# Both parts of a unit of weights in one tile, the parts at byte offsets chosen by kind of unit

## The chip, the core and the metric

The kernel runs on one core of a Trainium2 chip. The metric is the device time of one execution in microseconds (us); before the change the median of three runs is 968.93 us (968.75 to 969.19).

## What is computed

One layer of a bidirectional encoder on 256 tokens of width 2048, in float32. Cut to what matters here:

```python
h = _rmsnorm(x, norm1_g)
proj = h @ w_in                                  # 2048 x 3072: q (12 heads), k, v (4 heads), u (512)
a = _rmsnorm(_window_attention(q, k, v, sink), attn_out_g)
f = _rmsnorm(_fourier_mix(u, w_fourier), fourier_out_g)
x = x + jnp.concatenate([a, f], axis=-1) @ w_out           # 2048 x 2048
up = _rmsnorm(x, norm2_g) @ w_up                           # 2048 x 11008
act = gelu(conv3(gate) + dw_b) * val                       # width 5504
x = x + act @ w_down                                       # 5504 x 2048
return _rmsnorm(x, normf_g)
```

Nearly all the arithmetic is in the products with `w_in`, `w_out`, `w_up` and `w_down`.

## The kernel before

**Units of weights.** All weights are read once, in units of 128 partitions x 2048 float32 (1 MB): 24 of `w_in` (4 for u, 4 for v, 16 for the heads of q and k), 16 of `w_out`, 86 of `w_up` (gate and value of 43 tiles of 128 features), and the units of `w_down`. A unit is loaded by SyncE's queue into one of three `raw` buffers (`load`, L134), and `split_parts` (L149) makes two tiles of it in the type that TensorE reads in one pass: `hi`, the rounded value, written by ScalarE (L163), and `lo`, the rest `raw - hi`, written by VectorE (L164). Each has three buffers. Activations are held in the same way as two parts. A product then takes three matmuls (hi by hi, hi by the activations' rest, lo by hi), accumulated in one PSUM bank.

**Three forms of product.** A matmul holds one operand of 128 x 128 in the array (loaded by a separate instruction, PEld in the profile, while the matmul before it still runs) and streams the other through it.

- *Weights that stay* (`still_weights`, L308; heads of q and k, and all of `w_up`; 102 units). For each of 16 blocks of 128 rows, the hi part of the weights stays and 512 columns stream by (both parts of the activations side by side, L313), then the lo part stays and 256 columns stream by (L314). What streams is `hT` (`hU` after the second norm).
- *Weights that stream* (`moving_weights`, L296, lines L302 to L304): u and v, with `hT` staying; `w_out`, with the `cat` tiles staying; the units of `w_down` behind the last groups (`ps_l`), with `act` tiles staying.
- *Products* (`by_parts`, L1005, lines L1009 to L1011): the first 32 tiles of `w_down` in four groups of features, by a scheme with seven products of sums of blocks for each half of the columns, 56 in all. Here too the weights stream and an operand `op_*` stays. `split_product` (L897) makes hi and lo of them (L905, L906) in the same two rings of tiles as the units.

The last four units (`split_last`, L1131) have their own tiles.

**Order.** It is written out by hand. `unit(i, work)` (L345) issues the matmuls of unit i, then the small work that was put `beside` it, then the split of unit i + 2, which also issues the load of a unit three further on (L166); from the second norm on, `ff_step` (L936) does the same along `items`, in which products stand alternately with units of `w_up`. So when unit i is in TensorE, unit i + 1 is split, and i + 2 is being split into the buffer that unit i - 1 has left.

**Where the tiles lie.** Pools and tiles are laid out in each partition in the order in which they are opened: the pool `base` (with `hT`), then `wp` (`raw`, `hi`, `lo`, a scratch tile), then the pools of the stages. In the built program every tile of `raw`, `hi` and `lo`, the `cat`, `act` and `op_*` tiles start 32 bytes behind a multiple of 128 bytes, and the four `hT` tiles 96 bytes behind one. All slices that a matmul reads are whole multiples of 512 bytes further on, so an operand keeps its tile's distance. In this text a matmul's *offset* is the distance between the starts of the operand that streams and of the operand that is loaded under it, modulo 128 bytes: 0 for `w_out`, the late units of `w_down` and the products, 64 for u and v and for all weights that stay.

Of the kernel before, what the change touches and what calls it, by code (L numbers as in the profile page):

```python
# [9 lines left out]
F32R = mybir.dt.float32r  # L10
# [3 lines left out]
P = 128  # L14
# [33 lines left out]
N_U, N_V, N_QK = 0, 4, 8  # L48
# [7 lines left out]
LAST = list(range(40, NF))  # L56
# [27 lines left out]
def block_kernel(  # L84
# [22 lines left out]
    wp = ctx.enter_context(tc.tile_pool(name="wp", bufs=1))  # L107
# [3 lines left out]
    def f32(ap):  # L111
        return ap.bitcast(F32)
# [2 lines left out]
        return pool.tile([P, 512], F32, tag=pool.name, name=name)  # L115


    units = [(w_in[i], 2048) for i in range(24)] + [(w_out[i], 2048) for i in range(16)]
    n_front = len(units)
    items, up_index = ff_items(), {}  # L120
    for n, it in enumerate(items):
        if it[0] == "product":
            continue
        up_index[n] = len(units)
        if it[0] in ("gate", "val"):
            units.append((w_up[2 * it[1] + (it[0] == "val")], 2048))
        elif it[0] == "down":
            units.append((w_down_late[4 * it[1] + it[2]], 2048))
        else:
            units.append((w_down_last[it[1]], 512 * len(LAST)))  # L130
    RAW = 3
    raws, halves = {}, {}

    def load(i, pieces=1):  # L134
        if i < len(units) and i not in raws:
            src, n = units[i]
            raws[i] = wp.tile([P, 2048], F32, tag="raw", name=f"raw{i}", bufs=RAW)
            m = n // pieces
            for p in range(pieces):
                s = slice(p * m, (p + 1) * m)  # L140
                nc.sync.dma_start(raws[i][:, s], src[:, s])
                yield

    def split(i, pieces=1):

        for _ in split_parts(i, pieces):
            pass

    def split_parts(i, pieces):  # L149
        if i >= len(units):  # L150
            return
        n = units[i][1]
        raw = raws[i]
        hi = wp.tile([P, 2048], F32R, tag="hi", name=f"hi{i}", bufs=3)
        lo = wp.tile([P, 2048], F32R, tag="lo", name=f"lo{i}", bufs=3)
        halves[i] = (hi, lo)
        m = n // pieces
        for p in range(pieces):
            s = slice(p * m, (p + 1) * m)
            if i == 0 and p == 0:  # L160
                nc.vector.tensor_copy(hi[:, s], raw[:, s])
            else:
                nc.scalar.activation(hi[:, s], raw[:, s], AF.Copy)  # L163
            nc.vector.tensor_tensor(lo[:, s], raw[:, s], f32(hi[:, s]), ALU.subtract)  # L164
            yield
        for _ in load(i + RAW):  # L166
            pass
        load_more(i + RAW)
# [24 lines left out]
    nc.scalar.activation(warm[:, 0:1], warm[:, 1:2], AF.Copy)  # L193

    first = load(0, 4)
    nc.scalar.dma_start(vec[:, 0:NK], vecs[:, 0:NK])
    load_x(0, 0, S)
# [5 lines left out]
    next(first)  # L203
    load_x(2)
    second = load(1, 4)
    next(second)
    next(second)
# [15 lines left out]
    def load_more(i):  # L223

        if i == 4:
            for c in range(2):
                nc.sync.dma_start(xs[c], x[:, :, c * 512 : (c + 1) * 512])
        if i == 5:
            for c in range(2, 4):
                nc.sync.dma_start(xs[c], x[:, :, c * 512 : (c + 1) * 512])  # L230
        if i == 6:
            nc.sync.dma_start(chan, c_chan)
            nc.sync.dma_start(wfs, wf)
            nc.sync.dma_start(pos, c_pos)
        if i == 7:
            nc.sync.dma_start(vec[:, NK:V_N], vecs[:, NK:V_N])
            nc.sync.dma_start(rel, c_rel)
# [115 lines left out]
    for c in range(4):  # L353
        t = base.tile([P, 4, 512], F32R, tag=f"hT{c}", name=f"hT{c}")
        hT.append(t)
    ps_u = [bank(mm, f"ps_u{b}") for b in range(2)]
    for k in range(NK):
        c, q = k // 4, k % 4
        if q == 0:
            parts = split_parts(c, 4 if c < 2 else 2)  # L360
        split_scaled(hk(k), xTc[k // 2][:, (k % 2) * S : (k % 2 + 1) * S], vcol(V_G1 + k))
        next(parts, None)
        hi, lo = halves[c]
        for b in range(2):
            moving_weights(
                hi, lo, 512, [k], hk, b, ps_u[b], k == 0, k == NK - 1, q0=q
            )
        if q == 3:
            for _ in parts:
                pass  # L370
            del halves[c]
# [384 lines left out]
    for n, (c, kq) in enumerate(OUT_ORDER):  # L756
        i = N_OUT + n
# [35 lines left out]
    parts = {}  # L793
# [91 lines left out]
    def weights_of(g, c, w):  # L885
        return w_down[(g * 2 + c) * 4 + "abcd".index(w)]

    def ring_load():
        if ring_next[0] < len(ring):
            key = ring[ring_next[0]]  # L890
            ring_next[0] += 1
            ring_tiles[key] = fp.tile([P, 2048], F32, tag="rawd", name="rawd%d%d%s" % key)
            nc.sync.dma_start(ring_tiles[key], weights_of(*key))
# [3 lines left out]
    def split_product(g, c, p):  # L897

        raw = {w: ring_tiles.get((g, c, w)) for w in "abcd"}
        x = ring_tiles["x"]  # L900
        src = {"P1": raw["a"], "N3": raw["d"], "P7": raw["b"], "P2": raw["c"]}.get(p, x)
        hi = wp.tile([P, 2048], F32R, tag="hi", name=f"hi_{p}_{g}{c}", bufs=3)
        lo = wp.tile([P, 2048], F32R, tag="lo", name=f"lo_{p}_{g}{c}", bufs=3)
        halves["product", g, c, p] = (hi, lo)
        nc.scalar.activation(hi, src, AF.Copy)  # L905
        nc.vector.tensor_tensor(lo, src, f32(hi), ALU.subtract)  # L906
        if p in ("P1", "P7", "N3", "P2"):
            ring_load()
        elif p == "N5":
            nc.gpsimd.dma_start(x, weights_of(g, c, "d"), accum_op=ALU.add)  # L910
        elif p == "P6":
            nc.gpsimd.dma_start(x, weights_of(g, c, "c"), accum_op=ALU.add)
        elif p == "N4" and (g, c) != (N_GROUPS - 1, 1):
            pending.append(lambda: first_sums(g + c, 1 - c))

    def first_sums(g, c):

        a, b = ring_tiles[g, c, "a"], ring_tiles[g, c, "b"]
        x = ring_tiles["x"] = fp.tile([P, 2048], F32, tag="sumw", name=f"sumw{g}{c}", bufs=1)
        nc.vector.tensor_tensor(x, a, b, ALU.add)  # L920
        nc.gpsimd.dma_start(b, weights_of(g, c, "d"), accum_op=ALU.add)

    def split_item(n):
        if n >= len(items):
            return
        it = items[n]
        if n in up_index:
            split(up_index[n])
            if pending:
                pending.pop(0)()  # L930
        else:
            while pending:
                pending.pop(0)()
            split_product(*it[1:])
# [153 lines left out]
    for n, it in enumerate(items):  # L1088
# [15 lines left out]
        if it[0] == "product":  # L1104
            kind, g, c, p = it
# [9 lines left out]
        else:  # L1115
            kind, g, c = it
            hi, lo = halves.pop(up_index[n])
# [11 lines left out]
    i = up_index[n]  # L1129
# [145 lines left out]
```

## Time and profile before

| what | value |
|---|---|
| median of three runs | 968.93 us |
| span of the profiled execution (first to last instruction) | 967.9 us, so about 1.0 us lies around it |
| granted TensorE clock, mean | 0.997 of full |
| 60 to 206 us: q, k and the attention | 861 matmuls, TensorE busy all the time |
| 206 to 270 us: output projection | 308 matmuls, TensorE busy all the time |
| 270 to 860 us: `w_up` and the products | 3171 matmuls, TensorE busy all the time |
| read from memory | 208.65 MB, 218 GB/s over the span |

Times in the profile's views are microseconds unless they are marked ns. In a view that groups instructions a row has line, engine, operation, the tile written and the tiles read, shapes and count, then the group's busy time in us and the mean of one in ns, then idle time in front of it and what ended it. In a view in order of time a row begins with its start and its length. Matmuls overlap in the records: one that streams 512 columns is listed with some 390 ns although the next starts some 230 ns later. The spacing of their starts is what the time is made of, and the two differ by the same 162 ns in all the groups that are used below.

### The profile page before, as it was taken

To read this page: it belongs to the slowest core of one execution; us is meant where nothing else is said; L and a number is where in the kernel's file an instruction comes from. 1 tells how busy PE (TensorE), PEld (TensorE's weight loads), DVE (VectorE), ACT (ScalarE), POOL (GpSimd) and SP (SyncE) were. 2 spreads that over 40 slices of the span, in tenths; PEclk is the share of its full clock that TensorE was granted. 3 is DMA by queue.
4 is the path that set the end of the run, shared out by engine and by line. 5 is a ranking of instruction groups with operands and counts; after the bars stand their busy time and mean duration, and the time that the engine had idled before them with its cause. 6 is when DMAs were issued, how large, how long until landed. Compare 5 with 4: busy or idle time off the path is not lost.

```text
span 967.9 us, 12808 instructions
## 1 busy us (share of the span) xinstructions
PE 958.3 (99%) x5089; PEld 821.8 (85%) x5089; DVE 745.5 (77%) x924; ACT 537.5 (56%) x654; POOL 44.5 (5%) x59
## 2 busy tenths in 40 slices
PE   9999999999999999999999999999999999999996
PEld 7788988888888888888888888888888888888885
DVE  5668877666666679886898877988878989888674
ACT  6746666545554456655555555565555755553534
POOL 0000000000000000000000000000000000000003
PEclk9999999999999999999999999999999999999998
DMA  9844434445545675978687797776977696766532
GB/s 318 338 175 168 166 139 152 153 174 198 194 174 210 234 243 182 263 254 265 217 261 226 235 285 256 237 241 218 282 249 244 208 283 212 230 234 212 196 131 87
DMA packets 33548, 211.59 MB, mean 219 GB/s; under 512 B 3792, under 2 KB 4304, under 8 KB 9424
## 3 DMA queue, kind: packets, MB, share of 16 engines
q1 hardware_dynamic: 29744, 184.54, 51.3%
q0 software_dynamic: 3600, 26.22, 14.4%
q8 instruction: 40, 0.66, 0.3%
q14 instruction: 20, 0.16, 0.0%
q10 hardware_dynamic: 144, 0.01, 0.0%
HBM read 208.65 MB, written 2.10 MB: 218 GB/s over the span
## 4 chain that ended last, share of the span: by engine, by line
PE 95%; DMA 2%; DVE 1%; ACT 1%; issue 0%; POOL 0%; ACTq 0%; POOLq 0%; SPq 0%
PE ps_gate L313 17%; PE ps_val L313 17%; PE ps_gate L314 8%; PE ps_val L314 8%; PE ps_q L313 5%; PE ps_P L1009 3%; PE ps_P L1011 3%; PE ps_P L1010 3%; PE ps_q L314 2%; PE ps_a L304 2%; PE ps_a L303 2%; PE ps_a L302 2%; PE ps_N L1009 2%; PE ps_N L1011 2%; PE ps_N L1010 2%; DMA raw<-in_w_in 2%
## 5 line engine op out<-in xcount | busy, mean ns | idle before, releaser
L164 DVE TENSOR_TENSOR lo<-raw,hi 128x2048 fp32r<-128x2048 f32 (+3 forms) x145 | 313.0, 2158 | 59.3 <-ACT hi L163 59.3
L163 ACT ACTIVATE hi<-raw 128x2048 fp32r<-128x2048 f32 (+3 forms) x144 | 261.7, 1817 | 64.5 <-PE ps_l L303 25.4
L313 PE MATMUL ps_gate<-hU,hi 128*128 128x512 f32 x688 | 242.9, 394 | 0.0
L313 PE MATMUL ps_val<-hU,hi 128*128 128x512 f32 x688 | 242.8, 394 | 0.0
L314 PE MATMUL ps_gate<-hU,lo 128*128 128x256 f32 x688 | 193.1, 281 | 0.0
L314 PE MATMUL ps_val<-hU,lo 128*128 128x256 f32 x688 | 193.1, 281 | 0.0
L313 PEld LDWEIGHTS ps_val<-hU,hi 128*128 128x128 f32 x688 | 129.4, 188 | 29.9
L313 PEld LDWEIGHTS ps_gate<-hU,hi 128*128 128x128 f32 x688 | 129.4, 188 | 29.9
L314 PEld LDWEIGHTS ps_gate<-hU,lo 128*128 128x128 f32 x688 | 129.0, 187 | 1.1
L314 PEld LDWEIGHTS ps_val<-hU,lo 128*128 128x128 f32 x688 | 128.9, 187 | 1.1
L798 ACT ACTIVATE ft_g<-ps_gate 128x256 f32<-128x256 f32 x43 | 16.5, 383 | 127.5 <-PE ps_gate L314 127.5
L798 ACT ACTIVATE ft_v<-ps_val 128x256 f32<-128x256 f32 x43 | 16.5, 383 | 96.8 <-PE ps_val L314 96.7
L313 PE MATMUL ps_q<-hT,hi 128*128 128x512 f32 x192 | 68.5, 397 | 0.0
L314 PE MATMUL ps_q<-hT,lo 128*128 128x256 f32 x192 | 54.0, 281 | 0.0
L1009 PE MATMUL ps_P<-hi_P,op_P 128*128 128x512 f32 x128 | 50.2, 392 | 0.0
L1011 PE MATMUL ps_P<-lo_P,op_P 128*128 128x512 f32 x128 | 50.1, 391 | 0.0
L1010 PE MATMUL ps_P<-hi_P,op_P 128*128 128x512 f32 x128 | 49.8, 389 | 0.0
L906 DVE TENSOR_TENSOR lo_N<-sumw,hi_N 128x2048 fp32r<-128x2048 f32 x16 | 36.6, 2289 | 10.2 <-ACT hi_N L905 10.2
L313 PEld LDWEIGHTS ps_q<-hT,hi 128*128 128x128 f32 x192 | 36.1, 188 | 8.0
L800 DVE TENSOR_TENSOR fa_g<-ps_gate,ft_g 128x256 f32<-128x256 f32 x43 | 18.1, 421 | 29.4 <-ACT ft_g L798 29.4
L302 PE MATMUL ps_a<-hi,cat 128*128 128x512 f32 x96 | 37.8, 394 | 0.0
L1009 PE MATMUL ps_N<-hi_N,op_N 128*128 128x512 f32 x96 | 37.7, 393 | 0.0
(317 smaller groups left out, 1594.3 us busy)
## 6 DMA issues: line engine op xcount, KB each, us to landing
raw<-in_w_up SPq DMA_DIRECT2D x86, 1024.0 KB, 5.0
raw<-in_w_in SPq DMA_DIRECT2D x21, 1024.0 KB, 4.9
raw<-in_w_out SPq DMA_DIRECT2D x16, 1024.0 KB, 4.7
sumw<-in_w_down POOLq DMA_DIRECT2D x16, 1024.0 KB, 8.7
raw<-in_w_down_late SPq DMA_DIRECT2D x8, 1024.0 KB, 4.9
raw<-in_w_down_last SPq DMA_DIRECT2D x4, 768.0 KB, 4.2
raw<-in_w_in SPq DMA_DIRECT2D x8, 256.0 KB, 6.7
xs<-in_x SPq DMA_DIRECT2D x4, 512.0 KB, 10.2
```

Source lines behind the costliest of these rows:

```text
L163: nc.scalar.activation(hi[:, s], raw[:, s], AF.Copy)
L164: nc.vector.tensor_tensor(lo[:, s], raw[:, s], f32(hi[:, s]), ALU.subtract)
L302: nc.tensor.matmul(ps, ah, wh, start=first and q == q0, stop=False)
L303: nc.tensor.matmul(ps, al, wh, start=False, stop=False)
L304: nc.tensor.matmul(ps, ah, wl, start=False, stop=last and q == q0 + len(kk) - 1)
L313: nc.tensor.matmul(ps, hi[:, s], h, start=k == 0, stop=False)
L314: nc.tensor.matmul(ps[:, 0:S], lo[:, s], h[:, 0:S], start=False, stop=k == NK - 1)
L798: nc.scalar.activation(tmp, ps[:, S : 2 * S], AF.Copy)
L906: nc.vector.tensor_tensor(lo, src, f32(hi), ALU.subtract)
L1009: nc.tensor.matmul(ps, o[:, 0, p, :], hi[:, s], start=first and p == 0, stop=False)
L1010: nc.tensor.matmul(ps, o[:, 1, p, :], hi[:, s], start=False, stop=False)
L1011: nc.tensor.matmul(ps, o[:, 0, p, :], lo[:, s], start=False, stop=last and p == 3)
```

## The change

Both parts of a unit now lie in one tile of 4096 + 128 float32 (16,896 bytes) of one ring `parts` with three buffers. The hi part starts `oh` floats behind the tile's start and the lo part 2048 + `ol` floats behind it, and a table gives the two by the kind of unit. The loads and their queue, the order of the instructions on each engine, and what TensorE waits for stay the same.

```diff
-    units = [(w_in[i], 2048) for i in range(24)] + [(w_out[i], 2048) for i in range(16)]
+    units = [(w_in[i], 2048, "first" if i < N_QK else "still") for i in range(24)]
+    units += [(w_out[i], 2048, "moving") for i in range(16)]
...
-            units.append((w_up[2 * it[1] + (it[0] == "val")], 2048))
+            units.append((w_up[2 * it[1] + (it[0] == "val")], 2048, "still"))
         elif it[0] == "down":
-            units.append((w_down_late[4 * it[1] + it[2]], 2048))
+            units.append((w_down_late[4 * it[1] + it[2]], 2048, "moving"))
         else:
-            units.append((w_down_last[it[1]], 512 * len(LAST)))
+            units.append((w_down_last[it[1]], 512 * len(LAST), "moving"))
...
+    PLACES = {"still": (0, 16), "first": (16, 16), "moving": (0, 0), "product": (28, 28)}
+
+    def parts_tile(name, place):
+        t = wp.tile([P, 2 * 2048 + 128], F32R, tag="parts", name=name, bufs=3)
+        oh, ol = PLACES[place]
+        return t[:, oh : oh + 2048], t[:, 2048 + ol : 4096 + ol]
...
-        hi = wp.tile([P, 2048], F32R, tag="hi", name=f"hi{i}", bufs=3)
-        lo = wp.tile([P, 2048], F32R, tag="lo", name=f"lo{i}", bufs=3)
-        halves[i] = (hi, lo)
+        hi, lo = halves[i] = parts_tile(f"parts{i}", place)
...
-        hi = wp.tile([P, 2048], F32R, tag="hi", name=f"hi_{p}_{g}{c}", bufs=3)
-        lo = wp.tile([P, 2048], F32R, tag="lo", name=f"lo_{p}_{g}{c}", bufs=3)
-        halves["product", g, c, p] = (hi, lo)
+        hi, lo = halves["product", g, c, p] = parts_tile(f"parts_{p}_{g}{c}", "product")
```

In the built program the three tiles of the ring start 32 bytes behind a multiple of 128, as `hi` and `lo` did; `hT` stays where it was; the tiles behind the ring move by 1536 bytes, which is a multiple of 512. With the offset as defined above (stream against what is loaded under it):

| kind | where hi and lo start, modulo 128 bytes | offset before | offset after |
|---|---|---|---|
| u, v ("first") | 96, 96 (the stream) | 64 | 0 |
| weights that stay | 32, 96 (loaded under `hT` at 96) | 64, 64 | 0 where lo is loaded (under the 512 columns of L313), 64 where hi is loaded (under the 256 columns of L314) |
| `w_out`, late `w_down` ("moving") | 32, 32 (the stream) | 0 | 0 |
| products | 16, 16 (the stream) | 0 | 112 |

A buffer of hi could be written again as soon as the last matmul on hi had ended, and one of lo after the last matmul on lo. Now ScalarE waits for the last matmul on either part before it writes the tile's hi part (L163, L905); VectorE's own wait there is gone, since it waits for ScalarE anyway. 75 of TensorE's 389 semaphore signals fall away.

More of the change, by code (lines that the diff above doesn't have):

```diff
@@ L125, in block_kernel @@
         if it[0] in ("gate", "val"):
-            units.append((w_up[2 * it[1] + (it[0] == "val")], 2048))
+            units.append((w_up[2 * it[1] + (it[0] == "val")], 2048, "still"))
         elif it[0] == "down":
-            units.append((w_down_late[4 * it[1] + it[2]], 2048))
+            units.append((w_down_late[4 * it[1] + it[2]], 2048, "moving"))
         else:
-            units.append((w_down_last[it[1]], 512 * len(LAST)))
+            units.append((w_down_last[it[1]], 512 * len(LAST), "moving"))
     RAW = 3
     raws, halves = {}, {}
+    PLACES = {"still": (0, 16), "first": (16, 16), "moving": (0, 0), "product": (28, 28)}
[3 more added lines that the diff above has]
+        return t[:, oh : oh + 2048], t[:, 2048 + ol : 4096 + ol]
     def load(i, pieces=1):
         if i < len(units) and i not in raws:
-            src, n = units[i]
+            src, n, _ = units[i]
             raws[i] = wp.tile([P, 2048], F32, tag="raw", name=f"raw{i}", bufs=RAW)
@@ L151, in split_parts @@
             return
-        n = units[i][1]
+        _, n, place = units[i]
         raw = raws[i]
-        hi = wp.tile([P, 2048], F32R, tag="hi", name=f"hi{i}", bufs=3)
-        lo = wp.tile([P, 2048], F32R, tag="lo", name=f"lo{i}", bufs=3)
-        halves[i] = (hi, lo)
+        hi, lo = halves[i] = parts_tile(f"parts{i}", place)
         m = n // pieces
```

## Prediction

> **What bounds the kernel now.** First the page: busy times, TensorE's slices with its clock, and the chain of work that ended last.
>
> ```profile
> PE 958.3 (99%) x5089; PEld 821.8 (85%) x5089; DVE 745.5 (77%) x924; ACT 537.5 (56%) x654; POOL 44.5 (5%) x59
> PEclk9999999999999999999999999999999999999998
> PE 95%; DMA 2%; DVE 1%; ACT 1%; issue 0%; POOL 0%; ACTq 0%; POOLq 0%; SPq 0%
> ```
>
> TensorE is busy in 958.3 of 967.9 us at full clock, and 95% of the chain is its own work. So the time is the number of matmuls times the spacing of their starts. No matmul is added or removed; what the change can move is that spacing. The second view is therefore the list of groups by form.
>
> ```profile
> L313 PE MATMUL ps_gate<-hU,hi 128*128 128x512 f32 x688 | 242.9, 394 | 0.0
> L313 PE MATMUL ps_val<-hU,hi 128*128 128x512 f32 x688 | 242.8, 394 | 0.0
> L314 PE MATMUL ps_gate<-hU,lo 128*128 128x256 f32 x688 | 193.1, 281 | 0.0
> L313 PE MATMUL ps_q<-hT,hi 128*128 128x512 f32 x192 | 68.5, 397 | 0.0
> L313 PE MATMUL ps_k<-hT,hi 128*128 128x512 f32 x64 | 22.8, 396 | 0.0
> L303 PE MATMUL ps_v<-hi,hT 128*128 128x512 f32 x32 | 12.6, 395 | 0.0
> L304 PE MATMUL ps_v<-lo,hT 128*128 128x512 f32 x32 | 12.6, 395 | 0.0
> L303 PE MATMUL ps_l<-hi,act 128*128 128x512 f32 x64 | 24.9, 389 | 0.0
> L304 PE MATMUL ps_l<-lo,act 128*128 128x512 f32 x64 | 24.9, 389 | 0.0
> L1146 PE MATMUL ps_e<-hi,act 128*128 128x512 f32 x21 | 8.2, 389 | 0.0
> L1147 PE MATMUL ps_e<-hi,act 128*128 128x256 f32 x6 | 1.7, 283 | 0.0
> ```
>
> All rows of 512 columns do the same work, and yet ps_v takes 395 ns and ps_l 389. Lines 303 and 304 are the same code for both; what differs is where the operands lie: offset 64 for v, 0 for the late units. The weights that stay, offset 64 too, show 394 to 397. The timeline turns this into spacings.
>
> ```profile
> 33.84 0.40 PE L302 MATMUL ps_v<-hi,hT 128*128 128x512 f32 x1
> 35.94 0.39 PE L302 MATMUL ps_v<-hi,hT 128*128 128x512 f32 x1
> ...
> 866.01 0.39 PE L302 MATMUL ps_l<-hi,act 128*128 128x512 f32 x1
> 871.45 0.39 PE L302 MATMUL ps_l<-hi,act 128*128 128x512 f32 x1
> ...
> 320.98 0.39 PE L313 MATMUL ps_gate<-hU,hi 128*128 128x512 f32 x1
> 325.93 0.40 PE L313 MATMUL ps_gate<-hU,hi 128*128 128x512 f32 x1
> ...
> 374.59 0.39 PE L313 MATMUL ps_val<-hU,hi 128*128 128x512 f32 x1
> 379.48 0.40 PE L313 MATMUL ps_val<-hU,hi 128*128 128x512 f32 x1
> ```
>
> Nine matmuls of v lie between the first two rows: 2.10 / 9 = 233.3 ns each. Between the next two lie 24 of ps_l: 5.44 / 24 = 226.7 ns. The 6.7 ns between them is the 6 ns between 395 and 389, so the listed duration less 162 ns is the spacing. The last four rows bound 14 pairs (L313 and L314) each, in one code at the same places: 4.95 / 14 = 353.6 ns in a unit at 320 us and 4.89 / 14 = 349.3 ns in one at 374 us. So the pairs keep one of two spacings, and neither is the best one that the other rows allow: 226.7 ns as in ps_l, and for 256 columns 281 to 283 less 162, so 120 ns: 346.7 together.
>
> I read this as a collision in the memory of TensorE's two reads, the stream and the weight load under it, that depends on their places: offset 0 is the good case and 64 costs up to 6.7 ns for 512 columns. The other reading, that hT's tile rather than its offset is slow, would give the same rows; I hold it less likely, since hT is slow in both roles, staying (v) and streaming (L313).
>
> **The change part by part.** *Weights that stay, 1632 pairs.* While the 512 columns of L313 stream from hT (96), the lo part is loaded; it moves to 96, offset 0. While the 256 columns of L314 stream, the next hi part is loaded, still at 32: offset 64 as now. For gate and value the first goes from 394 to 389, -5 ns. L314 shows 281 at offset 64 and its like 282 to 283 at offset 0, so nothing is to be gained there; I take +1 ns, because a tighter pair keeps to 120. That is 1376 x -4 = -5.5 us. The 256 matmuls of q and k show 396 to 397, -7.5 + 1 = -6.5 ns, -1.7 us. Of this some 0.9 us isn't the placement's: the first matmul of most of these units takes longer behind the attention's transposes.
>
> ```profile
> 153.56 0.48 PE L313 MATMUL ps_q<-hT,hi 128*128 128x512 f32 x1
> 153.87 0.28 PE L314 MATMUL ps_q<-hT,lo 128*128 128x256 f32 x1
> ```
>
> This one has 310 ns to the next instead of 231, some 80 ns that stay; in all 16 units it would be 1.3 us, and I take two thirds. So q and k give -0.8 us, and this part -6.3 us. Bounds: from the spacing that each pair has to 346.7 it cannot exceed -1632 x 5 = -8.2 us by these rows; on the other side all pairs could fall to 353.6 ns, which costs those that stand at 349.3 now 4.3 ns each. If that is all units of `w_up` behind the 19 that have run by 374 us, 67 x 16 = 1072 pairs, it is +4.6 us.
>
> *u and v, 192 matmuls.* Offset 64 becomes 0: 395 to 389. For v 96 x -6 = -0.6 us. For u as much, but the beginning waits on loads (the chain's DMA 2%), which gives part back: -0.2 us. Sum -0.8 us; bounds 0 and -1.2.
>
> *w_out and the late units, 576 matmuls.* Offset 0 before and after: nothing.
>
> *Products, 672 matmuls.* The stream moves to 16, offset 112, which no matmul of 512 columns here has.
>
> ```profile
> L1009 PE MATMUL ps_P<-hi_P,op_P 128*128 128x512 f32 x128 | 50.2, 392 | 0.0
> L1010 PE MATMUL ps_P<-hi_P,op_P 128*128 128x512 f32 x128 | 49.8, 389 | 0.0
> L1011 PE MATMUL ps_P<-lo_P,op_P 128*128 128x512 f32 x128 | 50.1, 391 | 0.0
> L1009 PE MATMUL ps_N<-hi_N,op_N 128*128 128x512 f32 x96 | 37.7, 393 | 0.0
> L1010 PE MATMUL ps_N<-hi_N,op_N 128*128 128x512 f32 x96 | 37.3, 389 | 0.0
> L1011 PE MATMUL ps_N<-lo_N,op_N 128*128 128x512 f32 x96 | 37.6, 392 | 0.0
> ```
>
> The first matmuls of each product run unevenly until they settle. Against 389 that is (3 + 0 + 2) x 128 + (4 + 0 + 3) x 96 = 1.3 us in all. Offset 112 is 16 bytes from 0 and 48 from 64, so the nearest row is 389, and a quarter of the way to 395 gives 390.5, about today's mean. I take 0; bounds -1.3 us (all at 389) and 4.0 - 1.3 = +2.7 us (all at 395).
>
> *The shared tile.* ScalarE's write of the hi part now waits for the last matmul on lo, one matmul or 0.23 us later at most.
>
> ```profile
> ACT hi L163 <- PE ps_l L303: 25.4, 8, 4.0
> 865.98 1.92 ACT L163 ACTIVATE hi<-raw 128x2048 fp32r<-128x2048 f32 x1 [0.33 <-PE ps_N L1010]
> 868.83 2.28 DVE L164 TENSOR_TENSOR lo<-raw,hi 128x2048 fp32r<-128x2048 f32 x1
> ```
>
> Behind it on ScalarE stand the next unit's small works, and for it waits VectorE's lo part. In the tight place shown, hi would end at 865.98 + 0.23 + 1.92 = 868.13, and the lo part starts only at 868.83, behind VectorE's earlier work: 0.7 us are left. Elsewhere the split of unit i + 2 starts while unit i runs, and has the whole of unit i + 1 (16 pairs, 5.6 us) behind it before TensorE needs it. So nothing; without that cover it would be 0.23 us a unit. The writes at shifted places could take ScalarE and VectorE longer, and no row shows such a shift; even 5% of VectorE's 745.5 us would stay under TensorE's 958.3.
>
> Sum: -6.3 - 0.8 = -7.1 us. The profiled span of 967.9 becomes 960.8; the median lies 1.0 us above its span, so 961.8 us.
>
> The Trainium skill speaks against any effect: "TensorE: Matmul & The Clock Gate", in Part 2 on issuing a matmul, gives TensorE two independent read ports and says that loading the next weights takes no bandwidth from the running matmul. By it the sum would be 0. The two spacings of ps_v and ps_l, 233.3 and 226.7 ns, do not agree with that unless something other than the weight load tells them apart.
>
> **The rivals.**
>
> *Nothing happens*: 968.9 us. The spacing would hang on the tile or on something periodic in the chip, not on the offset. For it: two spacings of L313 at the same places (353.6 and 349.3). Against it: v stays at 395 in both its lines while ps_l, ps_e stay at 389. This is what the page's rule of the separate ports gives.
>
> *The pairs lock at the wider spacing*: slower. A pair now alternates offsets 0 and 64 where it had 64 and 64; if the phase that L313 leaves collides in L314, every pair takes 353.6 ns, +4.6 us, and the products at 395 add 2.7: 968.9 + 7.3 = 976 us. It decides once L314 gains more than 4 ns over 281 while L313 falls to 389. For it: the 349.3 ns came from the same code, so the phase counts and not the offset alone; a product with another offset hands the units behind it another phase. Against: L314 stands at 281 over both spacings, so it does not rise where L313 falls.
>
> *More than the best row*: one more step of 6.7 ns off L313 and the products, (1632 + 672) x 6.7 = 15.4 us further, 946 us. 512 columns at 226.7 ns still contain an overhead of which the rows do not show the bottom. Against: 24 matmuls in a row at offset 0 never go below.
>
> **How the numbers follow.** Forecast 0.62, nothing 0.10, wider spacing 0.18, more 0.10. The forecast's own range comes from the bounds of its parts: -8.2 - 1.2 - 1.3 gives 958 us, and the products at +2.7 with another 1 ns on every L314 (1.6 us) give 966. To hold eight in ten, the range takes in no effect and the mildest part of the wider spacing above, and half of the extra step below: 954 to 971 us. About 0.2% (1.9 us) is what a measurement of this kernel can tell from no change. Faster: the forecast and the extra step, 0.62 + 0.10 = 0.72; same 0.10; slower 0.18.
>
> **What would show it.** In the profile after: L303 and L304 of ps_v at 389; L313 of gate and value at 389 to 390 and L314 at 281 to 282; rows of ps_l as before; the products' three lines between 389 and 392. Fourteen pairs of a gate unit should take 4.85 us in every part of the run. ScalarE's waits on TensorE for L163 should name the lo lines and be a little longer, with no gap in TensorE behind them. I am wrong if ps_v keeps 395 (then the offset is not the cause), if L314 rises by what L313 falls, or if the products exceed 395.

## The result and the profile after

The changed kernel takes 967.21 us (median of 20 runs, 966.56 to 968.01) against 969.22 us before (20 runs, 968.62 to 969.73). The ratio is 0.998, with a 95% interval of 0.9973 to 0.9987: 2.0 us faster, where the forecast was 7.1 us. The time lies within the range of 954 to 971 us, far from the 961.8 us that it was put at.

The page of the changed kernel: span, busy times, and the chain that ended last.

```profile
span 965.3 us, 12801 instructions
PE 955.1 (99%) x5089; PEld 820.1 (85%) x5089; DVE 745.0 (77%) x924; ACT 540.0 (56%) x654; POOL 44.6 (5%) x59
PE 98%; DMA 1%; ACT 0%; SPq 0%; POOL 0%; issue 0%; DVE 0%; ACTq 0%; POOLq 0%
```

TensorE still sets the end, so the spacing of matmuls is again the place to look. The groups by form, with the changed kernel's line numbers: L320 and L321 are L313 and L314 of before, L310 and L311 are L303 and L304, L1014 to L1016 are L1009 to L1011.

```profile
L320 PE MATMUL ps_gate<-hU,parts 128*128 128x512 f32 x688 | 242.2, 394 | 0.0
L321 PE MATMUL ps_gate<-hU,parts 128*128 128x256 f32 x688 | 192.7, 280 | 0.0
L320 PE MATMUL ps_q<-hT,parts 128*128 128x512 f32 x192 | 66.9, 393 | 0.0
L321 PE MATMUL ps_q<-hT,parts 128*128 128x256 f32 x192 | 53.2, 277 | 0.0
...
L310 PE MATMUL ps_v<-parts,hT 128*128 128x512 f32 x32 | 12.5, 389 | 0.0
L311 PE MATMUL ps_v<-parts,hT 128*128 128x512 f32 x32 | 12.5, 389 | 0.0
L310 PE MATMUL ps_l<-parts,act 128*128 128x512 f32 x64 | 24.9, 389 | 0.0
...
L1014 PE MATMUL ps_P<-parts_P,op_P 128*128 128x512 f32 x128 | 50.2, 392 | 0.0
L1015 PE MATMUL ps_P<-parts_P,op_P 128*128 128x512 f32 x128 | 50.9, 398 | 0.0
L1016 PE MATMUL ps_P<-parts_P,op_P 128*128 128x512 f32 x128 | 49.6, 387 | 0.0
```

ps_v fell from 395 to 389 as forecast and ps_l stayed. But the hi matmul of gate still shows 394, and in the products one line rose to 398. The timeline says more than these means. First the unit gate30 and the head q3 of the changed kernel, the first row and the one 14 pairs on:

```profile
702.30 0.39 PE L320 MATMUL ps_gate<-hU,parts 128*128 128x512 f32 x1
707.20 0.40 PE L320 MATMUL ps_gate<-hU,parts 128*128 128x512 f32 x1
...
88.57 0.39 PE L320 MATMUL ps_q<-hT,parts 128*128 128x512 f32 x1
93.33 0.39 PE L320 MATMUL ps_q<-hT,parts 128*128 128x512 f32 x1
```

Gate30 takes 4.90 / 14 = 350.0 ns a pair, q3 takes 4.76 / 14 = 340.0, and the code and the places modulo 128 bytes are the same. 340 is less than the 346.7 that the forecast took as the best. Unit by unit, 9 of the 16 units of q and k, gate0, val0 and the last six units of `w_up` settle at 340; the other seven units of q and k run at 350, and so do all 78 units from gate1 to val39. The start of gate1:

```profile
271.67 0.61 PE L293 MATMUL ps_spread<-diag,ones 128*128 128x128 f32 x4
272.03 0.47 PE L320 MATMUL ps_gate<-hU,parts 128*128 128x512 f32 x1
272.35 0.28 PE L321 MATMUL ps_gate<-hU,parts 128*128 128x256 f32 x1
272.46 0.40 PE L320 MATMUL ps_gate<-hU,parts 128*128 128x512 f32 x1
272.70 0.28 PE L321 MATMUL ps_gate<-hU,parts 128*128 128x256 f32 x1
272.81 0.40 PE L320 MATMUL ps_gate<-hU,parts 128*128 128x512 f32 x1
```

Behind the four small matmuls of `spread` the first matmul takes 320 ns. From the second pair on every pair takes 350 without a transition (348 or 349 for the first pair behind a product), up to val39, some 580 us later. Behind val39 come late units of `w_down`, and the next unit of `w_up`, gate40, settles at 340 in its fourth pair.

Summed over the distances of starts in both traces, this is where the time went, beside what the prediction had set down:

| part | forecast, us | measured, us |
|---|---|---|
| `w_up`, 1376 pairs | -5.5 | -1.3 |
| q and k, 256 pairs | -0.8 | -1.8 |
| v; u, which waits on loads | -0.8 | -0.6; -0.7 |
| `w_out`, late units | 0 | 0.0 |
| products, 672 matmuls | 0 | +1.7 |
| sum | -7.1 | -2.7 (span: 967.9 to 965.3) |

### The profile page after: what moved, and what is told of

The parts are those of the page before. It is cut to its first block, busy times and chain, and to the rows that moved or that the text cites. A ratio compares the mean times of both kernels' runs of the same rounds, so it can differ in the third digit from the quotient of the medians.

```text
span 965.3 us, 12801 instructions
## 1 busy us (share of the span) xinstructions
PE 955.1 (99%) x5089; PEld 820.1 (85%) x5089; DVE 745.0 (77%) x924; ACT 540.0 (56%) x654; POOL 44.6 (5%) x59
## 4 chain that ended last, share of the span: by engine, by line
PE 98%; DMA 1%; ACT 0%; SPq 0%; POOL 0%; issue 0%; DVE 0%; ACTq 0%; POOLq 0%
PE ps_val L320 16%; PE ps_gate L320 16%; PE ps_gate L321 8%; PE ps_val L321 8%; PE ps_q L320 5%; PE ps_P L1015 3%; PE ps_P L1014 3%; PE ps_P L1016 3%; PE ps_N L1015 2%; PE ps_q L321 2%; PE ps_N L1014 2%; PE ps_a L311 2%; PE ps_a L309 2%; PE ps_a L310 2%; PE ps_N L1016 2%; PE ps_k L320 2%
## 5 line engine op out<-in xcount | busy, mean ns | idle before, releaser
L171 DVE TENSOR_TENSOR parts<-raw,parts 128x2048 fp32r<-128x2048 f32 (+3 forms) x145 | 313.0, 2159 | 63.7 <-ACT parts L170 63.5
L170 ACT ACTIVATE parts<-raw 128x2048 fp32r<-128x2048 f32 (+3 forms) x144 | 262.0, 1819 | 75.4 <-PE ps_l L311 25.7
L320 PE MATMUL ps_gate<-hU,parts 128*128 128x512 f32 x688 | 242.2, 394 | 0.0
L320 PE MATMUL ps_val<-hU,parts 128*128 128x512 f32 x688 | 242.2, 394 | 0.0
L321 PE MATMUL ps_gate<-hU,parts 128*128 128x256 f32 x688 | 192.7, 280 | 0.0
L321 PE MATMUL ps_val<-hU,parts 128*128 128x256 f32 x688 | 192.7, 280 | 0.0
L320 PEld LDWEIGHTS ps_val<-hU,parts 128*128 128x128 f32 x688 | 129.3, 188 | 29.8
L320 PEld LDWEIGHTS ps_gate<-hU,parts 128*128 128x128 f32 x688 | 129.3, 188 | 29.7
L321 PEld LDWEIGHTS ps_gate<-hU,parts 128*128 128x128 f32 x688 | 129.2, 188 | 1.1
L321 PEld LDWEIGHTS ps_val<-hU,parts 128*128 128x128 f32 x688 | 129.1, 188 | 1.1
L320 PE MATMUL ps_q<-hT,parts 128*128 128x512 f32 x192 | 66.9, 393 | 0.0
L321 PE MATMUL ps_q<-hT,parts 128*128 128x256 f32 x192 | 53.2, 277 | 0.0
L1015 PE MATMUL ps_P<-parts_P,op_P 128*128 128x512 f32 x128 | 50.9, 398 | 0.0
L1014 PE MATMUL ps_P<-parts_P,op_P 128*128 128x512 f32 x128 | 50.2, 392 | 0.0
L1016 PE MATMUL ps_P<-parts_P,op_P 128*128 128x512 f32 x128 | 49.6, 387 | 0.0
L320 PEld LDWEIGHTS ps_q<-hT,parts 128*128 128x128 f32 x192 | 36.1, 188 | 7.3
## 6 DMA issues: line engine op xcount, KB each, us to landing
xs<-in_x SPq DMA_DIRECT2D x4, 512.0 KB, 10.7
```

Source lines behind the costliest of these rows:

```text
L320: nc.tensor.matmul(ps, hi[:, s], h, start=k == 0, stop=False)
L321: nc.tensor.matmul(ps[:, 0:S], lo[:, s], h[:, 0:S], start=False, stop=k == NK - 1)
L1014: nc.tensor.matmul(ps, o[:, 0, p, :], hi[:, s], start=first and p == 0, stop=False)
L1015: nc.tensor.matmul(ps, o[:, 1, p, :], hi[:, s], start=False, stop=False)
L1016: nc.tensor.matmul(ps, o[:, 0, p, :], lo[:, s], start=False, stop=last and p == 3)
```

## The experiments

All kernels start from the changed one unless it is said otherwise. The edits are cut to the lines that matter, and an edit that is only described repeats one shown before it. The two theories were: *A*, the spacing is a phase between the stream and the weight loads, which a matmul inherits from the one before; the places only decide which spacings there are. *B*, the spacing is settled by the places and by how a stage starts, and a product in between does not alter it. Times are medians with the ratio to the kernel before the change and its 95% interval, where there was more than one run.

### The products back at offset 0

```diff
-    PLACES = {..., "product": (28, 28)}
+    PLACES = {..., "product": (0, 0)}
```

> As the changed kernel, but the products' parts back at offset 0. In the changed kernel a pair of the weights that stay takes either 350.0 ns (233 + 117) or 340.0 ns (227 + 113), and keeps what it has from unit to unit; a product at offset 112 takes 231.3 ns a matmul against 228.6 before. Theory A (a unit hands its phase on, and the products at 112 hand on the 350): the products go back to some 228.6, -1.8 us, and from the first product on the units of w_up run at 340, 1072 pairs x -10 ns = -10.7 us; 967.2 - 12.5 = 954.7 us. Theory B (the 350 comes from the start of w_up and no product alters it): the pairs stay at 350.0, only the products gain; 965.4 us.

957.8 us, ratio 0.9882 (0.9867 to 0.9897). The timeline of this kernel: val8, the last unit but one ahead of the first product (its first row and the one 14 pairs on), and val9, the first unit behind that product (from its second pair to 14 pairs on).

```profile
357.43 0.40 PE L320 MATMUL ps_val<-hU,parts 128*128 128x512 f32 x1
362.33 0.39 PE L320 MATMUL ps_val<-hU,parts 128*128 128x512 f32 x1
...
371.76 0.39 PE L320 MATMUL ps_val<-hU,parts 128*128 128x512 f32 x1
376.53 0.39 PE L320 MATMUL ps_val<-hU,parts 128*128 128x512 f32 x1
```

4.90 / 14 = 350.0 ns ahead of it, 4.77 / 14 = 340.7 behind. The 17 units from gate1 to gate9 stay at 350; all from the first product on settle at 340. The units of `w_up` themselves were not touched: a product decides what they take. Theory B is out. The total is 3 us above theory A's 954.7. Summed over starts, `w_up` takes 8.4 us less than in the changed kernel where 10.7 were expected: the last six units had stood at 340 already (1.0 us), and a unit behind a product needs three pairs until it stands at 340 (its first ones take 350, 346 and 345), which makes up most of the rest; the products give 1.4 us of 1.8, at 229 to 230 ns a matmul; and u took 1.5 us more in this trace, with its loads.

### The shared tile alone

```diff
+    PLACES = {"still": (0, 0), "first": (0, 0), "moving": (0, 0), "product": (0, 0)}
```

> The shared tile alone, all parts at the tile's own places (offsets as before the change). If only places count, pairs at 349 to 353 ns, v at 395 ns listed, products at 389 to 393, and 969.2 us as before. If the shared tile's later release of the buffer costs time, it is above 970 us with waits of ScalarE that TensorE follows.

969.11 us, ratio 0.9998 (0.9988 to 1.0007). Summed over starts, v, q and k, `w_up`, `w_out` and the products differ from the kernel before by 0.0 us each (u by 0.5, with its loads). The tile and its later release cost nothing that can be measured, as the prediction had it, and the effect lies in the places.

### Both loads of the weights that stay at offset 0

```diff
+    PLACES = {"still": (16, 16), "first": (16, 16), "moving": (0, 0), "product": (0, 0)}
```

> As e1_product0, but both parts of the weights that stay at 96, so that both loads are at offset 0. Theory A with offset 0 as the good case for either load: 340.0 ns or less in every unit, at or below e1_product0. If the load under 256 columns wants offset 64, as the change has it, the pairs are above 340 and the kernel is slower than e1_product0.

965.69 us, ratio 0.9962 (0.9947 to 0.9977): slower than with lo alone moved, so theory A's 340 ns or less did not come. The pairs of gate30:

```profile
701.69 0.39 PE L320 MATMUL ps_gate<-hU,parts 128*128 128x512 f32 x1
706.55 0.39 PE L320 MATMUL ps_gate<-hU,parts 128*128 128x512 f32 x1
```

4.86 / 14 = 347.1 ns between these two, and 346.7 as the mean of most units: the figure that the prediction put together from ps_l and the 256 columns at offset 0. That sum was right for `w_up` with offset 0 under both loads, but the change does not have that. These places have two spacings as well: in 11 of the 16 units of q and k the pairs settle at 353 to 355. With the load under the 256 columns at 64, as in the change, a pair is faster than 346.7 in one phase (340) and slower in the other (350).

### Only the products moved

```diff
+    PLACES = {"still": (0, 0), "first": (0, 0), "moving": (0, 0), "product": (28, 28)}
```

> Only the products moved (offset 112), all else at the old offsets. The products alone cost 672 x (231.3 - 228.6) = +1.8 us by theory B, 971.0 us. By theory A they also decide the spacing of the pairs behind them, which stood at 353 before the first product and at 349 behind it: if they hand on the wider one, 1072 x 4.3 = +4.6 us more, 975.6 us.

974.73 us, ratio 1.0053 (1.0036 to 1.007). By form, gate in this kernel:

```profile
L320 PE MATMUL ps_gate<-hU,parts 128*128 128x512 f32 x688 | 244.5, 395 | 0.0
L321 PE MATMUL ps_gate<-hU,parts 128*128 128x256 f32 x688 | 193.8, 282 | 0.0
```

The units of `w_up` lie where they did before the change, yet they now stand at 353 ns behind the first product as well, up to val39, where they had been at 349: the products hand on the wider spacing, at +3.3 us there and +1.9 us in the products. Theory A's 975.6 was close.

### Eight more matmuls ahead of gate1

```diff
+        if n == 2:
+            nhi, nlo = halves[up_index[n]]
+            ps = bank(mm, "ps_extra")
+            for k in range(8):
+                nc.tensor.matmul(
+                    ps, nlo[:, k * P : (k + 1) * P], hT[0][:, 0, :], start=True, stop=True
+                )
```

With the products at offset 0:

> As e1_product0, with eight more matmuls of 512 columns at offset 0 (the next unit's lo blocks under the first block of hU, into a bank that nobody reads) ahead of the unit gate1, where the pairs fall to 350. They cost 8 x 227 ns = 1.8 us. If a pair's spacing is the phase that it inherits (theory A), the 18 units up to the first product go from 350 to 340: 288 x -10 ns = -2.9 us, 957.8 - 1.1 = 956.7 us. If the early units are at 350 for another cause (what the other engines do there), they stay, and it is 959.6 us.

956.34 us, ratio 0.9871 (0.9854 to 0.9887), and the units from gate1 to the first product, 17 of them and not the 18 of the expectation, stand at 340. With the products as the change has them, at 112:

> The changed kernel (products at offset 112) with the same eight matmuls. Theory A says that gate1 and the units up to the first product take 340. Behind the products two readings differ: if the products at 112 only keep the phase that they find, all 85 units stay at 340, some 967.2 + 1.8 - 2.9 - 10.7 = 955.4 us; if they set it to the wider spacing, the units behind them go back to 350 and it is 966.1 us.

954.6 us in the one run: more work, 12.6 us less time. The start of gate1 in this kernel, then gate30 (14 pairs apart), then its products by form:

```profile
272.68 2.08 PE L1102 MATMUL ps_extra<-hU,parts 128*128 128x512 f32 x8
274.59 0.40 PE L320 MATMUL ps_gate<-hU,parts 128*128 128x512 f32 x1
...
693.48 0.39 PE L320 MATMUL ps_gate<-hU,parts 128*128 128x512 f32 x1
698.24 0.39 PE L320 MATMUL ps_gate<-hU,parts 128*128 128x512 f32 x1
...
L1014 PE MATMUL ps_P<-parts_P,op_P 128*128 128x512 f32 x128 | 49.8, 389 | 0.0
L1015 PE MATMUL ps_P<-parts_P,op_P 128*128 128x512 f32 x128 | 49.8, 389 | 0.0
L1016 PE MATMUL ps_P<-parts_P,op_P 128*128 128x512 f32 x128 | 49.8, 389 | 0.0
```

4.76 / 14 = 340.0 ns through the whole stage, and these products fall to 389 in all three lines, without a transition (one product, at 808 us, lost 0.4 us). So the products at 112 do not make the wide spacing: they keep what they find, the good phase (226.7 ns) or the bad one (231, 237.5 and 225 in turn). The changed kernel lost at one place, the start of gate1, and its products carried the loss through 78 units.

### Places of the weights that stay, one pair of places a unit

```diff
+    SCAN = [(a, b + 32 * (b < a)) for a in (0, 16, 28, 8, 24, 4, 12, 20) for b in range(0, 32, 4)]
+    SCAN = [(0, 16)] + [c for c in SCAN if c != (0, 16)]
+    for n, it in enumerate(items):
+        if it[0] in ("gate", "val") and n and items[n - 1][0] == "product" and SCAN:
+            i = up_index[n]
+            units[i] = (*units[i][:2], SCAN.pop(0))
...
+    PLACES = {"still": (0, 16), "first": (16, 16), "moving": (0, 0), "product": (0, 0)}
...
+        oh, ol = PLACES.get(place) or place
```

> As e1_product0, but each of the 55 units of w_up that come right behind a product has places of its own (all in steps of 16 bytes, 128 more for lo where it would meet hi), so that the spacing of a pair is read unit by unit. Theory A with the offset as cause: the unit at (0, 16) at 340 to 341, those like (0, 0) at 349, like (16, 16) at 346.7, the others between 340 and 360, the same for lo places that differ by 128 bytes. If the offset does not count, all are at one value. No place below 340 would say that this is the floor. The sum over mixed places says nothing of itself; some 962 us.

964.2 us. Mean of a pair in its unit, once the unit has settled, from the starts in the trace (places of hi and lo in floats modulo 32):

```
(0,16)  340.0     (0,0)  348.9     (16,16) 346.7     (16,0) 346.7
(0,4)   346.7     (0,8)  348.9     (0,12)  353.3     (0,20) 353.3
(8,8)   346.7     (16,20) 353.3    (24,16) 353.4     (28,28) 346.7
```

Of 55 pairs of places that were read, one stands at 340: the change's own. All others lie between 346 and 354. With lo moved by 16 bytes to either side of (0,16), the pair is among the worst (353.3), so a distance is no measure here. Each place was read in one unit, and with what came before it: at the change's own places a unit can stand at 350 too, so another place may have a narrower spacing that this run did not meet.

### Places of the products, one pair of places a product

```diff
+    SCAN = [(a, b + 32 * (b < a)) for a in (0, 16, 28, 8, 24, 4, 12, 20) for b in range(0, 32, 4)]
...
-        hi, lo = halves["product", g, c, p] = parts_tile(f"parts_{p}_{g}{c}", "product")
+        hi, lo = halves["product", g, c, p] = parts_tile(f"parts_{p}_{g}{c}", SCAN.pop(0) if SCAN else "product")
```

> As e1_product0, but each of the 56 products has places of its own in steps of 16 bytes. Read unit by unit: (0, 0) should give some 229 ns a matmul, (28, 28) 231.3, and if the distance on a circle of 128 bytes counts, as the prediction took it for 112, the worst is 64 at 233 or more. If 112 is bad because it is no multiple of 64, then all odd multiples of 16 bytes are as bad as 112. What the units of w_up behind each product take (340 or 350) shows which places hand on the wide spacing.

959.6 us. Mean of a product's twelve matmuls: (28,28) 226.7, with every one at 226 or 227 from the first on; next (16,16) and (12,28) at 228.9; (0,0) 230.9 in its transition; most others 230 to 234. The prediction's guess, an effect that grows with the distance from offset 0, does not fit: (28,28) and (4,4) both lie 16 bytes from it and take 226.7 and 231.8. Nor does the other reading in the expectation: (12,12) and (4,4), odd multiples of 16 bytes too, stand at 230.0 and 231.8 and not at 226.7. Each place was read in one product, in the phase that it met. The units behind the products mostly stood at 340, and behind seven places, (0,20), (0,28), (8,12), (8,20), (4,8), (4,28) and (12,4), at 350.

### The blocks of one unit in another order, and fewer extra matmuls

The unit gate1 alone takes its first four hi blocks in a row, then their lo blocks, then pairs (`lead` is 4 there and 0 elsewhere):

```diff
-    def still_weights(hi, lo, ps, kk):
+    def still_weights(hi, lo, ps, kk, lead=0):
-        for k in kk:
+        kk = list(kk)
+        steps = [(k, p) for p in range(2) for k in kk[:lead]]
+        steps += [(k, p) for k in kk[lead:] for p in range(2)]
+        for k, p in steps:
...
-            still_weights(*halves.pop(up_index[n]), ps, range(NK))
+            still_weights(*halves.pop(up_index[n]), ps, range(NK), 4 if n == 2 else 0)
```

> The changed kernel with no work added: the unit gate1 alone takes its first four hi blocks one after the other and then their lo blocks, before it goes on in pairs. Theory A: four matmuls of 512 columns in a row move the phase as the eight extra ones did, at no cost; all units of w_up at 340 and the products at 226.7 ns, 954.6 - 1.8 = 952.8 us. If the four hi loads at offset 64 lead back to the same phase, the units stay at 350 and it is 967.2 us. A value between would mean that the phase is lost again on the way.

953.14 us, ratio 0.9836 (0.9819 to 0.9852), with the same number of matmuls as before. Its start of gate1, and TensorE's busy time on the page:

```profile
271.86 1.17 PE L324 MATMUL ps_gate<-hU,parts 128*128 128x512 f32 x4
272.87 0.64 PE L326 MATMUL ps_gate<-hU,parts 128*128 128x256 f32 x4
273.35 0.39 PE L324 MATMUL ps_gate<-hU,parts 128*128 128x512 f32 x1
273.58 0.28 PE L326 MATMUL ps_gate<-hU,parts 128*128 128x256 f32 x1
273.69 0.39 PE L324 MATMUL ps_gate<-hU,parts 128*128 128x512 f32 x1
...
PE 940.5 (99%) x5089; PEld 813.0 (86%) x5089; DVE 744.6 (78%) x924; ACT 540.1 (57%) x654; POOL 44.5 (5%) x59
```

Eight matmuls after the start a pair takes 273.69 - 273.35 = 0.34 us, and the next 77 units settle at the same. This also sets aside another cause for the gain of the extra matmuls: they took a PSUM bank, so that all later results lay one bank further on, and here no bank moves. Two extra matmuls in place of eight:

> The changed kernel with two extra matmuls ahead of gate1 where there were eight. If the phase needs only a step, 954.6 - 6 x 0.227 = 953.2 us; if it has to settle over several matmuls, as the first ten or so of the late units of w_down do, the units stay at 350: 967.2 + 0.5 = 967.7 us.

953.2 us in the one run: a step is enough, the phase doesn't need to settle first. The same order also at the seven units of q and k that stood at 350:

> As e9_order, with the same order of the first four blocks in the seven units of q and k that stand at 350 in the changed kernel (the four k, and the heads 1, 7, 10). If the order turns them, 7 x 16 x -10 ns = -1.1 us against e9_order; if the order at the head of a unit does nothing, both kernels are alike, at 967.2.

952.04 us, ratio 0.9825 (0.981 to 0.9839). Against the kernel with gate1 alone in another order this is inside the scatter of the runs (951.93 to 953.5 there, 951.58 to 953.02 here). The traces tell more: all seven units turned to 340, but two whose code was not touched, q0 and q4, went from 340 to 350; summed over starts, q and k take 0.6 us less where 1.1 were expected. The last one is the control, on the kernel before the change:

> The kernel before the change with the eight extra matmuls, as a control of what they do where the places are the old ones. They cost 1.8 us; if they move the 18 early units from 353 to 349, -288 x 4.3 ns = -1.2 us: 969.9 us; if they move nothing, 971.1 us. Anything below 968 would say that the extra matmuls help by themselves and not through the new places.

971.4 us. The eight matmuls cost their time and change nothing there; `w_up` differs by 0.1 us. The extra blocks lie at offset 64 here and at 0 in the kernels above, so this run does not show that no step could turn the phase at the old places. A turn there would be worth little by the rows of before: 17 units from 353.6 to 349.3 ns are 1.2 us. The new places alone gave 2.0 us, and the new places with the other phase 16 us.

## Why the prediction was wrong

*TensorE's spacing is the only thing that moves: right.* The sum over starts, -2.7 us, is the span's difference, -2.6. ScalarE's wait moved to the lo line and grew by 0.3 us in eight cases together, behind TensorE's work as said:

```profile
ACT parts L170 <- PE ps_l L311: 25.7, 8, 4.0
```

*Places count, and hT's tile is not to blame: right.* v went from 233 to 227 ns when its weights moved and hT stayed. In the three runs that kept the old places of v (the shared tile alone, only the products moved, and the control) it takes 22.8 us as before, in all others 22.2 to 22.3. The Trainium skill says in "TensorE: Matmul & The Clock Gate", Part 2 ("What happens when you issue a matmul"), that loading the next weights takes no read bandwidth from the running matmul, and the prediction derived a sum of 0 from it. The sum is not 0: the same instructions take 340 to 354 ns a pair by nothing but the places and the phase. Whether the weight load is what slows the matmul, no run shows.

*u and v, -0.8 us: right for v*, -0.6. For u, -0.7 was measured, but its sum moves by more than that from trace to trace with its loads (24.2 to 25.9 us at the new places, 24.6 to 25.8 at the old ones), so the gain of u is not shown.

*Weights that stay, -6.3 us: the step that failed.* It let the offset alone set each matmul's cost: 394 to 389 ns under offset 0, no gain at 64, so that the new places would replace the two spacings of before, 353.6 and 349.3, by one best value, 346.7 in every unit. In fact these places have spacings of their own and the phase picks one: 353 and 349 at the old places, 350 and 340 at the new. In 78 of the 86 units of `w_up` it was 350, and the gate's 512 columns stayed at 394. The prediction had the sign of it in the rival of the wider spacing ("the phase counts and not the offset alone; a product with another offset hands the units behind it another phase"), but priced it with the old values. Its term of +1 ns for L314 was wrong in sign too: 256 columns fell from 119 or 120 to 117 ns in the wide case, and to 113 in the narrow one, which is below any row of before. By chance q and k, where 340 is common, gave more than forecast (-1.8 against -0.8), and `w_up`, which was caught at 350, gave -1.3 of -5.5.

*Products, 0 us: mis-sized, and for a wrong reason.* The nearest row was taken by distance in bytes. In the bad phase the three lines take 231, 237.5 and 225 ns (+1.7 us); in the good one 226.7 each, and the sum is 1.0 us below the kernel before. The bounds, -1.3 to +2.7, hold both. One line is listed at 398 (by starts 237.5, so that listed time and spacing differ by 160.5 ns here and not by 162), over the 395 that the prediction had named as a sign that it was wrong.

*The reading of the two spacings.* The prediction saw in the rows of before that one code at the same places had two spacings, and that they changed once between 320 and 374 us, where the first product stands. Asking there what had changed at that moment would have pointed to a value that is handed on, and so to the start of `w_up`, behind the small matmuls of `spread`, as the place that decides the change's worth. How much hung on it, 967 us or 953, only the experiments show.

What stays open: why a start behind small matmuls leads to the one phase or the other (of the units of q and k, some run at 350 and some at 340 behind the same kind of work), and what the phase is a phase of: that the stream and the weight load collide in the memory contradicts no row here, but no run measured it by itself. No run took `spread` away from ahead of gate1.

## What to carry to other kernels

Where matmuls follow each other without a pause, the spacing of their starts shows whether operands' places cost something: compare groups with the same shape, then units of one group over time. If one code shows two spacings, look for the place where it changes and what ran just before, and read a new layout's worth only in units that began in the same phase. A layout can look worth 0.2% because of one bad start; a few blocks in another order there were worth 1.4% more.

## What the runs showed of the hardware

A pair of matmuls (512 and 256 columns, each with its own weights) kept one of two spacings, 350.0 or 340.0 ns, through 78 units and some 580 us, across products in between, and took the other after two extra matmuls (953.2 us against 967.2). Three matmuls of a product, at the places of the change, did the same with 231.3 or 226.7 ns on average. Moving the streamed operand by 64 bytes took v from 233 to 227 ns. In the scan, with one unit for each place, the pair stood at 340 ns with lo at (0,16) and at 353 with lo 16 bytes to either side, at (0,12) and (0,20).
